# A hybrid encoder block on one core: one output run per half, independent stores in the inverse, head sums by two float32r products, and late places for two tiles

## The chip, the cores and the metric

The kernel runs on one core of a Trainium2 chip. The core has five engines, each with an instruction queue of its own that is worked in order: TensorE (PE, with its weight loads shown apart as PEld), VectorE (DVE), ScalarE (ACT), GpSimd (POOL) and SyncE (SP, which here only issues transfers). Engines wait for each other by semaphores. The metric is the device time of one execution in microseconds (us); lower is better.

## The reference

One layer of an encoder block on x of 1024 tokens by 1024 channels, in float32: two branches run side by side on the same normed input (stick-breaking attention and an RWKV-7 time mix), a gated merge, then a SwiGLU feed-forward part. The diff touches the time mix, 8 heads of 64 channels:

```python
kk = (k * k_k).reshape(B, S, H, N)
kk = kk / jnp.maximum(jnp.linalg.norm(kk, axis=-1, keepdims=True), 1e-12)   # a sum over a head
k = k * (1.0 + (a - 1.0) * k_a)
y = wkv7_scan(r_h, heads(decay), k_h, v_h, kk, heads(a))
mean = jnp.mean(y, axis=-1, keepdims=True)
var = jnp.mean(jnp.square(y - mean), axis=-1, keepdims=True)                # a sum over a head
y = ((y - mean) * lax.rsqrt(var + GN_EPS)).reshape(B, S, RW_WIDTH) * lnx_w + lnx_b
bonus = (jnp.sum(r_h * k_h * r_k, axis=-1, keepdims=True) * v_h)            # a sum over a head
return (y + bonus) * g
```

`wkv7_scan` steps a 64x64 state per head over the tokens: `sa = state @ -kk; state = state * w + sa (kk a)^T + v k^T; y = state @ r`.

## The kernel before

**Data.** Activations stand with channels on the 128 partitions and tokens along the rows. Products that need nearly float32 accuracy are made of three float32r products of parts: a value is cast to float32r (`hi`, on ACT) and the remainder taken (`lo = x - hi`, on DVE); `mm3` multiplies hi by hi, hi by lo, lo by hi.

**The time mix.** `rwkv` goes over four pairs of heads `p` (two heads fill 128 partitions) and two halves `hf` of 512 tokens: eight units. For each unit:

- `rw_elementwise` makes the operands from r, k, v. Two sums over each head, one for the norm of `kk` (`pn`) and one for the bonus (`pb`), are products with a 128x128 matrix of two blocks of ones (`b.ones`), in float32 with 512 columns. It masks products into `nx` (four chunks a tile), spreads v into `sv`, and copies blocks of it by DMA into `xv`.
- `rw_inverse` inverts a triangular 32x32 block per chunk, head and quarter: 31 steps of a multiply and a reduce on DVE (tiles `nl`, `ts`, `tm`), four stores of the result into a scratch in HBM (`td`), one load back in another order (`dt`), a 32x32 transpose on DVE, then small products on PE, 32 rows by 32 columns of the array, and 64 by 64 right after in `rw_elementwise`.
- `rw_chain` runs over eight chunks of 64 tokens. A chunk has two dependent 128x128 float32 products (`px`, then `ps`) with copies (`xv`), a scaled state (`sp`, on POOL) and the new state (`sv`, on DVE) between them. After chunks 3 and 7, four chunks' outputs are added into `y` by 8 products of 64x64 and 8 of 128x64, kept together.
- `rw_post` norms y, with a third sum over each head (`pn`), multiplies by the gate `g` loaded from HBM, and stores the half.

Projections for the next pair and gate tiles (`gate_tiles`) are recorded beside the chain as filler for PE: float32r products of 512 columns into PSUM tiles `d`.

**What sets the order.** Nothing runs in the order of the code. `Block` records every operation, and `schedule` lays them out by a list plan: each engine takes the able operation with the lowest priority number, at times that it reckons from `cost` and from `LATENCY` (from one engine's end to another's start), to which `wait` adds 80 ns between different engines. The finished order is what each engine's queue holds; the chip then waits only for semaphores. All instructions are issued from one helper line, L579 of the profile, so groups are told apart by tiles. An operation that must follow another is found by the boxes of memory that both touch (`regions`); for a scratch in HBM with strided boxes these may be wider than what is touched, so the four stores of `td`, which interleave, count as one after the other. For a transfer the planner reckons:

```python
    "sync": {"tensor": 2030, "vector": 2030, "scalar": 2030, "gpsimd": 2060, "sync": 2030},
...
    size = 4 * count(out.shape)
    return max(450.0, size / 360.0)
```

`choose` has a rule of its own for PE: after an operation that costs under 70 it prefers another such. These are small products; going from one array shape (rows x columns of the array in use) to another costs time, which `run` reckons by `array_mode` (INTO_PART 90, INTO_WHOLE 200). `together()` keeps a bundle's products adjacent.

**Places.** A tile gets a place of its class (`b`: 27 places of 1040 float32 per partition, each able to hold two small tiles) when the planner grants it. A tile may ask ahead of its turn within a window, 60 tiles for `b` or, with `near=True`, 12 (`PREFETCH`). A place that holds small tiles keeps in the profile the name of the one that took it first, so a sum's input may be listed as `b_gg`, `b_sh` or `b_tmp`.

Of the kernel before, what the change touches and what calls it, by code (L numbers as in the profile page):

```python
# [6 lines left out]
F32 = mybir.dt.float32  # L7
F32R = mybir.dt.float32r
BF16 = mybir.dt.bfloat16
AF = mybir.ActivationFunctionType  # L10
ALU = mybir.AluOpType
# [4 lines left out]
P = 128  # L16
# [3 lines left out]
H = 512  # L20
# [13 lines left out]
CH = 64  # L34
# [7 lines left out]
CC_ID, CC_CEN, CC_ONE, CC_MA, CC_TI, CC_SC, CC_N = 0, 128, 256, 384, 512, 768, 1280  # L42
# [214 lines left out]
class Block:  # L257
# [272 lines left out]
    def choose(self, able, waiting, at, last):  # L530


        import heapq

        if able[0][2].engine == "tensor" and waiting and waiting[0][3].steady:

            x = waiting[0]
            if x[0] <= at + 3 and x[1] < able[0][0]:
                heapq.heappop(waiting)
                return x[3]  # L540
        if able[0][2].engine == "tensor" and last is not None and last.cost < 70:
            short = [x for x in able if x[2].cost < 70]
            if short:
                pick = min(short)
                able.remove(pick)
                heapq.heapify(able)
                return pick[2]
        return heapq.heappop(able)[2]
# [59 lines left out]
    def proj(self, w, hf, cls="d"):  # L608
# [4 lines left out]
        return ps  # L613


    def rstd(self, srcs, junk):
# [25 lines left out]
def hybrid_block(tc, x, w_in, consts, params, rows, ups, gup, w_sb, w_rw, w_o, w_fg, w_fu, w_fd, out):  # L642
    b = Block(tc, {a.tensor.name for a in (x, w_in, consts, params, rows, ups, gup, w_sb, w_rw, w_o, w_fg, w_fu, w_fd)})
    nc = b
    T = b.t
    with ExitStack() as es:
# [8 lines left out]
        b.cls("sp", 3, CH)  # L655
        b.cls("q", 4, 256)
        b.cls("big", 4, 4 * S)
        for n in ("raw", "whi", "wlo"):
# [15 lines left out]
        for i, cls in enumerate("dd"):  # L674
            ps = T(cls, [P, H])
# [15 lines left out]
        b.cen = cst[:, CC_CEN : CC_CEN + P]  # L691
        b.ones = cst[:, CC_ONE : CC_ONE + P]
        b.mask_a = cst[:, CC_MA : CC_MA + P]
# [196 lines left out]
def rw_elementwise(b, u, p, hf, spill):  # L890
    nc = b.nc
    T = b.t
    pc, oka, cen, ones, mask_a, tinit = b.pc, b.oka, b.cen, b.ones, b.mask_a, b.tinit
    r, k, v = u["r"], u["k"], u["v"]
# [22 lines left out]
    nc.scalar.activation(t0[:], k[:], AF.Square, scale=pc(PC_KK + p))  # L917
    pn = T("e", [P, H])
    nc.tensor.matmul(pn[:], lhsT=ones, rhs=t0[:], start=True, stop=True)
    rn = T("b", [P, H], F32, "tmp")  # L920
# [22 lines left out]
    nc.vector.scalar_tensor_tensor(out=rk[:], in0=r[:], scalar=pc(PC_RK + p), in1=kp[:], op0=ALU.mult, op1=ALU.mult)  # L943
    pb = T("e", [P, H])
    nc.tensor.matmul(pb[:], lhsT=ones, rhs=rk[:], start=True, stop=True)
    bv = T("b", [P, H], F32, "bv")
# [36 lines left out]

    xv = T("b", [P, 8, P], F32, "xv")
    u["xv"] = xv
# [31 lines left out]
def rw_inverse(b, nd, nx, quads, tinit, p, hf):  # L1017
# [10 lines left out]
    for t in range(1, 32):  # L1028
        n = (t + 3) // 4
        nc.vector.tensor_tensor(out=tm[:, :n, : t + 1], in0=nl[:, None, 0 : t + 1, t].broadcast_to([P, n, t + 1]), in1=ts[:, :n, : t + 1], op=ALU.mult)  # L1030
        nc.vector.tensor_reduce(out=ts[:, :n, t], in_=tm[:, :n, : t + 1], axis=AX.X, op=ALU.add)
    td = b.scratch([32, 8, 4, 32], f"td{p}{hf}")
    for c in range(4):
        nc.sync.dma_start(td[:, :, c, :], ts[c:P:4])
    dt = T("q", [P, 8, 32])
    nc.sync.dma_start(dt[:], td.rearrange("(c a) j k t -> (a j k) c t", a=4))
# [26 lines left out]
def rw_chain(b, units, p, hf):  # L1063
# [6 lines left out]
    hs = [(0, slice(0, CH)), (1, slice(CH, P))]  # L1070
    y = None
    for c in range(8):
# [10 lines left out]
        if not last:  # L1083
# [3 lines left out]
            for h, rs in hs:  # L1087
                nc.vector.scalar_tensor_tensor(out=nsv[rs, ncx, rs], in0=ps[rs, rs], scalar=pl[rs, c : c + 1], in1=sp[rs, :], op0=ALU.mult, op1=ALU.add)
        if c % 4 == 3:
            g = c // 4  # L1090
            if y is None:
                y = u["y"] = T("y", [P, H])
            with b.together():
                for k in range(4 * g, c + 1):
                    for h, rs in hs:
                        nc.tensor.matmul(y[rs, k * CH : k * CH + CH], lhsT=sv[rs, k, rs], rhs=ar[rs, k, CH:P], start=k == 0, stop=False, skip_group_check=True)
                for k in range(4 * g, c + 1):
                    for h, rs in hs:
                        nc.tensor.matmul(y[rs, k * CH : k * CH + CH], lhsT=xv[:, k, rs], rhs=nx[g][:, k % 4, 1, h, :], start=False, stop=k == 7, skip_group_check=True)


def rw_post(b, u, p, hf, spill):
    nc = b.nc
    T = b.t
    pc, ones = b.pc, b.ones
    y, t0 = T("b", [P, H], F32, "ptmp"), T("b", [P, H], F32, "ptmp")
    nc.scalar.copy(y, u["y"])
    nc.scalar.activation(t0[:], y[:], AF.Square)
    pn = T("c", [P, H])
    nc.tensor.matmul(pn[:], lhsT=ones, rhs=t0[:], start=True, stop=True)  # L1110
    rs = T("b", [P, H], F32, "ptmp")
    nc.scalar.activation(rs[:], pn[:], AF.Ln, scale=1.0 / CH, bias=b.eps[:, 1:2])
    nc.scalar.activation(rs[:], rs[:], AF.Exp, scale=-0.5)
    nc.vector.scalar_tensor_tensor(out=rs[:], in0=y[:], scalar=pc(PC_LW + p), in1=rs[:], op0=ALU.mult, op1=ALU.mult)
    nc.vector.scalar_tensor_tensor(out=rs[:], in0=rs[:], scalar=pc(PC_LB + p), in1=u["bv"][:], op0=ALU.add, op1=ALU.add)
    g = T("b", [P, H], F32, "ptmp")
    nc.sync.dma_start(g[:], spill["g"][:])
    nc.gpsimd.tensor_tensor(out=rs[:], in0=rs[:], in1=g[:], op=ALU.mult)
    nc.sync.dma_start(b.orw_d[p][:, hf * H : hf * H + H], rs[:])
# [533 lines left out]
```

## Time and profile before

| | |
|---|---|
| Runs | 1610.81 us median of 3 (1609.73 to 1612.65) |
| Profiled execution | 1610.57 us, its span 1608.8 us |
| Instructions | 23912 |
| Granted TensorE clock | 0.999 mean |
| HBM | 129.27 MB read, 47.45 MB written, 110 GB/s over the span |

The rows are quoted in the prediction. In the table of groups, the columns are line, engine, operation, out<-in by the tiles' names, partitions x elements and type, count, then the busy time in us, the mean ns of one, and the engine's idle time just before them with what ended it. A matmul row has the array's rows x columns in use ahead of the shape. A float32 product is two records, a float32r one is one. A matmul's record runs from its start to its modelled end, so records of neighbours overlap: what a product takes of PE's time is read from the start of the next one.

### The profile page before, as it was taken

To read this page: it belongs to the slowest core of one execution; us is meant where nothing else is said; L and a number is where in the kernel's file an instruction comes from. 1 tells how busy PE (TensorE), PEld (TensorE's weight loads), DVE (VectorE), ACT (ScalarE), POOL (GpSimd) and SP (SyncE) were. 2 spreads that over 40 slices of the span, in tenths; PEclk is the share of its full clock that TensorE was granted. 3 is DMA by queue.
4 is the path that set the end of the run, shared out by engine and by line. 5 is a ranking of instruction groups with operands and counts; after the bars stand their busy time and mean duration, and the time that the engine had idled before them with its cause. 6 is when DMAs were issued, how large, how long until landed. Compare 5 with 4: busy or idle time off the path is not lost.

```text
span 1608.8 us, 23912 instructions
## 1 busy us (share of the span) xinstructions
PE 1586.0 (99%) x8932; PEld 1284.1 (80%) x8932; DVE 1128.0 (70%) x2004; ACT 716.5 (45%) x1401; POOL 254.5 (16%) x407
## 2 busy tenths in 40 slices
PE   9999999999999999999999999999999999999998
PEld 7877777777787888888787888888888888888876
DVE  7568689897864878895366349766666666867485
ACT  7533345444245766774444334323332332554352
POOL 1030233525233222230043110000000000000000
PEclk9999999999999999999999999999999999999999
DMA  5523233242321000003537112332232233874444
GB/s 214 203 88 92 79 100 86 59 140 83 105 71 40 27 27 27 27 27 122 180 118 274 66 40 81 116 98 98 99 111 89 95 111 124 310 240 144 136 152 183
DMA packets 106822, 180.38 MB, mean 112 GB/s; under 512 B 42321, under 2 KB 43345, under 8 KB 106706
## 3 DMA queue, kind: packets, MB, share of 16 engines
q1 hardware_dynamic: 106706, 178.85, 33.6%
q8 instruction: 70, 1.15, 0.3%
q14 instruction: 46, 0.38, 0.1%
HBM read 129.27 MB, written 47.45 MB: 110 GB/s over the span
## 4 chain that ended last, share of the span: by engine, by line
PE 86%; DVE 7%; ACT 3%; DMA 3%; issue 1%; POOL 0%; SPq 0%; DVEq 0%; ACTq 0%; POOLq 0%
PE d_d L579 39%; PE e_e L579 20%; PE c_c L579 16%; PE y_y L579 10%; DVE q_q L579 2%; DVE b_sv L579 1%; DMA b_wraw<-w_fd 0%; DVE big_h L579 0%; DVE b_xs L579 0%; ACT b_qst L579 0%; DMA q_q<-td 0%; DVE wlo_wlo L579 0%; DMA whi_oraw<-w_o 0%; DMA b_g<-gsc 0%; DVE b_nx L579 0%
## 5 line engine op out<-in xcount | busy, mean ns | idle before, releaser
L579 PE MATMUL d_d<-big_h,whi_whi 128*128 128x512 f32 x1280 | 434.5, 409 | 0.1
L579 PEld LDWEIGHTS d_d<-big_h,whi_whi 128*128 128x128 f32 x1280 | 234.9, 189 | 48.7 <-issue 5.5
L579 PE MATMUL d_d<-big_h,wlo_wlo 128*128 128x512 f32 x640 | 259.9, 406 | 0.0
L579 PEld LDWEIGHTS d_d<-big_h,wlo_wlo 128*128 128x128 f32 x640 | 120.7, 189 | 24.6 <-issue 2.4
L579 DVE TENSOR_TENSOR q_q<-b_nl,q_q 128x2 f32<-128x2 f32 (+30 forms) x248 | 86.5, 349 | 9.9 <-POOL b_sh L579 2.4
L579 ACT CAST whi_whi<-raw_raw 128x1024 fp32r<-128x1024 f32 (+1 forms) x60 | 55.9, 933 | 77.5 <-PE d_d L579 76.4
L579 DVE TENSOR_TENSOR_SCAN b_nb<-b_nb 128x128 f32<-128x128 f32 (+3 forms) x64 | 87.9, 1390 | 1.7 <-POOL b_nb L579 1.0
L579 DVE TENSOR_TENSOR wlo_wlo<-raw_raw,whi_whi 128x1024 fp32r<-128x1024 f32 (+1 forms) x60 | 69.5, 1160 | 27.4 <-ACT whi_whi L579 27.3
L579 POOL TENSOR_SCALAR sp_sp<-b_sv,pl_pl 64x64 f32<-64x64 f32 x120 | 63.3, 528 | 121.9 <-DVE b_sv L579 115.9
L579 ACT CAST b_wd<-b_wraw 128x512 fp32r<-128x512 f32 x70 | 42.1, 620 | 64.4 <-DVE b_wraw L579 30.0
L579 DVE TENSOR_REDUCE q_q<-q_q 128x1 f32<-128x2 f32 (+30 forms) x248 | 62.1, 250 | 6.8
L579 PE MATMUL d_d<-b_wd,big_act 128*128 128x512 f32 x264 | 66.5, 395 | 0.0
L579 PE MATMUL e_e<-b_wd,big_act 128*128 128x512 f32 x264 | 66.5, 394 | 0.0
L579 DVE TENSOR_TENSOR b_wd<-b_wraw,b_wd 128x512 fp32r<-128x512 f32 x70 | 46.4, 686 | 27.0 <-ACT b_wd L579 27.0
L579 POOL TENSOR_SCALAR_AFFINE_SELECT b_nb<-b_nb 128x128 f32<-128x128 f32 x64 | 45.4, 716 | 123.5 <-ACT b_nb L579 108.4
L579 PEld LDWEIGHTS e_e<-b_wd,big_act 128*128 128x128 f32 x264 | 49.6, 188 | 11.8
L579 PEld LDWEIGHTS d_d<-b_wd,big_act 128*128 128x128 f32 x264 | 49.6, 188 | 11.7
L579 DVE TENSOR_TENSOR b_wt<-c_c,b_wt 128x512 fp32r<-128x512 f32 (+2 forms) x96 | 50.0, 546 | 3.8 <-ACT b_wt L579 2.7
L579 ACT CAST b_wt<-c_c 128x512 fp32r<-128x512 f32 (+2 forms) x96 | 43.5, 481 | 20.5 <-PE c_c L579 19.5
L579 ACT COPY b_xv<-c_c 64x64 f32<-64x64 f32 x64 | 13.3, 207 | 86.2 <-DVE b_xv L579 46.0
L579 PE MATMUL c_c<-b_wd,big_act 128*128 128x512 f32 x198 | 50.8, 395 | 0.1
L579 PE MATMUL y_y<-b_wd,big_act 128*128 128x512 f32 x198 | 50.7, 394 | 0.0
(648 smaller groups left out, 3576.4 us busy)
## 6 DMA issues: line engine op xcount, KB each, us to landing
raw_raw<-w_in SPq DMA_DIRECT2D x42, 512.0 KB, 3.5
raw_raw<-w_fg SPq DMA_DIRECT2D x22, 512.0 KB, 3.5
raw_raw<-w_fu SPq DMA_DIRECT2D x22, 512.0 KB, 3.6
b_wraw<-w_fd SPq DMA_DIRECT2D x22, 512.0 KB, 4.7
act<-b_u SPq DMA_DIRECT2D x39, 256.0 KB, 3.1
b_x<-x SPq DMA_DIRECT2D x16, 512.0 KB, 9.0
b_mg<-gsc SPq DMA_DIRECT2D x28, 256.0 KB, 5.3
raw_araw<-act SPq DMA_DIRECT2D x14, 512.0 KB, 4.5
```

What stands on the lines that cost most here:

```text
L579: getattr(getattr(self.real, op.engine), op.method)(**kw)
```

## The change

1. `head_sums` replaces each of the three float32 products with the ones: the input is cast to float32r on ACT, the remainder taken on DVE, and two float32r products add into one PSUM tile. The ones themselves are copied once to float32r on ACT, at the start.
2. The outputs of a half are made in one bundle after chunk 7: 16 products of 64x64, then 16 of 128x64.
3. The four stores of `td` are taken out of each other's list of predecessors in the planner.
4. `xv` and the gate tile `g` get `near=True`.
5. `choose` prefers operations that use fewer than 128 rows of the array after one that did, in place of those that cost under 70.

```diff
-        if able[0][2].engine == "tensor" and last is not None and last.cost < 70:
-            short = [x for x in able if x[2].cost < 70]
+        if able[0][2].engine == "tensor" and last is not None and array_mode(last)[0] < P:
+            short = [x for x in able if array_mode(x[2])[0] < P]
...
+    def head_sums(self, cls, x):
+        nc = self.nc
+        both = self.t("b", [P, 2, H], F32R, "hs")
+        hi, lo = both[:, 0], both[:, 1]
+        nc.scalar.copy(hi, x)
+        nc.vector.tensor_tensor(out=lo, in0=x, in1=hi, op=ALU.subtract)
+        ps = self.t(cls, [P, H])
+        nc.tensor.matmul(ps, lhsT=self.ones, rhs=hi, start=True, stop=False)
+        nc.tensor.matmul(ps, lhsT=self.ones, rhs=lo, start=False, stop=True)
+        return ps
...
-        b.ones = cst[:, CC_ONE : CC_ONE + P]
+        b.ones = T("ones", [P, P], F32R)
+        nc.scalar.copy(b.ones, cst[:, CC_ONE : CC_ONE + P])
...
-    pn = T("e", [P, H])
-    nc.tensor.matmul(pn[:], lhsT=ones, rhs=t0[:], start=True, stop=True)
+    pn = b.head_sums("e", t0)
...
-    xv = T("b", [P, 8, P], F32, "xv")
+    xv = T("b", [P, 8, P], F32, "xv", near=True)
...
+    stores = set()
     for c in range(4):
         nc.sync.dma_start(td[:, :, c, :], ts[c:P:4])
+        b.ops[-1].preds -= stores
+        stores.add(b.ops[-1])
...
-        if c % 4 == 3:
-            g = c // 4
-            if y is None:
-                y = u["y"] = T("y", [P, H])
-            with b.together():
-                for k in range(4 * g, c + 1):
...
+    y = u["y"] = T("y", [P, H])
+    with b.together():
+        for k in range(8):
...
-    g = T("b", [P, H], F32, "ptmp")
+    g = T("b", [P, H], F32, "ptmp", near=True)
```

(`pb` in `rw_elementwise` and `pn` in `rw_post` change as `pn` above.)

The first head sum of the first unit on PE, among projections. `d_d` is a projection's output, `big_h` the normed input, `whi` and `wlo` a weight's parts; `b_gg` is here the place of the squared k. Before:

```order
L579 MATMUL d_d_967<-big_h_200,whi_whi_863 128x512
L579 MATMUL d_d_967<-big_h_214,whi_whi_863 128x512
L579 MATMUL d_d_967<-big_h_200,wlo_wlo_871 128x512
L579 MATMUL e_e_997<-b_gg_721,cst_cst_146 128x512
L579 MATMUL d_d_1001<-big_h_192,whi_whi_934 128x512
L579 MATMUL d_d_1001<-big_h_208,whi_whi_934 128x512
```

After:

```order
L579 MATMUL d_d_974<-big_h_202,whi_whi_868 128x512
L579 MATMUL d_d_974<-big_h_216,whi_whi_868 128x512
L579 MATMUL d_d_974<-big_h_202,wlo_wlo_876 128x512
L579 MATMUL e_e_1005<-b_hs_859,ones_ones_166 128x512 x2
L579 MATMUL d_d_1010<-big_h_194,whi_whi_941 128x512
L579 MATMUL d_d_1010<-big_h_210,whi_whi_941 128x512
```

The sum stands at the same place, as two products with the float32r ones.

The first outputs of the first chain on PE (`b_ar`, `b_sv`, `b_nx`, `b_xv` as above). Before, after chunk 3; rows of the same two forms stand again after chunk 7:

```order
L579 MATMUL d_d_1843<-big_h_208,whi_whi_1658 128x512
L579 MATMUL c_c_1849<-b_xv_1053,b_bkt_1202 128x128
L579 MATMUL y_y_1852<-b_ar_915,b_sv_1010 64x64 x8
L579 MATMUL y_y_1852<-b_nx_1158,b_xv_1053 64x64 x8
L579 MATMUL d_d_1843<-big_h_192,wlo_wlo_1670 128x512
L579 MATMUL c_c_1881<-b_sv_1010,b_nx_1184 128x128
```

After, once, behind chunk 7:

```order
L579 MATMUL d_d_1959<-big_h_194,whi_whi_1879 128x512
L579 MATMUL c_c_1985<-b_xv_1053,b_bkt_1239 128x128
L579 MATMUL y_y_1989<-b_ar_922,b_sv_1020 64x64 x16
L579 MATMUL y_y_1989<-b_nx_1179,b_xv_1053 64x64 x8
L579 MATMUL y_y_1989<-b_nx_1219,b_xv_1053 64x64 x8
L579 MATMUL d_d_1959<-big_h_210,whi_whi_1879 128x512
```

Two runs have become one of double length.

The fifth inverse's transfers on SP (`td` the scratch, `q_q` the inverse's tiles, `gsc` gates, `raw` weights, `orw` a half's result). Before:

```order
L579 DMA td_120<-q_q_2845 256x1x32 x2
L579 DMA orw_83<-b_ptmp_1004 128x512
L579 DMA gsc_70<-b_tmp_3678 128x512
L579 DMA td_120<-q_q_2845 256x1x32
L579 DMA raw_raw_3762<-w_in 128x1024
L579 DMA td_120<-q_q_2845 256x1x32
L579 DMA b_tmp_3678<-g_d_107 128x512
L579 DMA gsc_71<-b_tmp_3682 128x512
L579 DMA q_q_3800<-td_120 128x8x32
```

After:

```order
L579 DMA raw_raw_3842<-w_in 128x1024
L579 DMA gsc_72<-b_k_2162 128x512
L579 DMA td_120<-q_q_2880 256x1x32 x4
L579 DMA gsc_72<-b_pp_2608 128x512
L579 DMA q_q_3925<-td_120 128x8x32
L579 DMA raw_raw_3929<-w_in 128x1024
```

Four stores stand in a row, and one gate's store between them and the load.

More of the change, by code (lines that the diff above doesn't have):

```diff
@@ L656, in hybrid_block @@
         b.cls("q", 4, 256)
+        b.cls("ones", 1, P)
         b.cls("big", 4, 4 * S)
@@ L892, in rw_elementwise @@
     T = b.t
-    pc, oka, cen, ones, mask_a, tinit = b.pc, b.oka, b.cen, b.ones, b.mask_a, b.tinit
+    pc, oka, cen, mask_a, tinit = b.pc, b.oka, b.cen, b.mask_a, b.tinit
     r, k, v = u["r"], u["k"], u["v"]
@@ L943, in rw_elementwise @@
     nc.vector.scalar_tensor_tensor(out=rk[:], in0=r[:], scalar=pc(PC_RK + p), in1=kp[:], op0=ALU.mult, op1=ALU.mult)
-    pb = T("e", [P, H])
-    nc.tensor.matmul(pb[:], lhsT=ones, rhs=rk[:], start=True, stop=True)
+    pb = b.head_sums("e", rk)
     bv = T("b", [P, H], F32, "bv")
@@ L1070, in rw_chain @@
     hs = [(0, slice(0, CH)), (1, slice(CH, P))]
-    y = None
     for c in range(8):
@@ L1088, in rw_chain @@
                 nc.vector.scalar_tensor_tensor(out=nsv[rs, ncx, rs], in0=ps[rs, rs], scalar=pl[rs, c : c + 1], in1=sp[rs, :], op0=ALU.mult, op1=ALU.add)
-        if c % 4 == 3:
-            g = c // 4
-            if y is None:
-                y = u["y"] = T("y", [P, H])
-            with b.together():
-                for k in range(4 * g, c + 1):
[L1095 to L1099, printed above, removed]
+    y = u["y"] = T("y", [P, H])
+    with b.together():
+        for k in range(8):
+            for h, rs in hs:
+                nc.tensor.matmul(y[rs, k * CH : k * CH + CH], lhsT=sv[rs, k, rs], rhs=ar[rs, k, CH:P], start=k == 0, stop=False, skip_group_check=True)
+        for k in range(8):
+            for h, rs in hs:
+                nc.tensor.matmul(y[rs, k * CH : k * CH + CH], lhsT=xv[:, k, rs], rhs=nx[k // 4][:, k % 4, 1, h, :], start=False, stop=k == 7, skip_group_check=True)
 def rw_post(b, u, p, hf, spill):
@@ L1104, in rw_post @@
     T = b.t
-    pc, ones = b.pc, b.ones
+    pc = b.pc
     y, t0 = T("b", [P, H], F32, "ptmp"), T("b", [P, H], F32, "ptmp")
@@ L1108, in rw_post @@
     nc.scalar.activation(t0[:], y[:], AF.Square)
-    pn = T("c", [P, H])
-    nc.tensor.matmul(pn[:], lhsT=ones, rhs=t0[:], start=True, stop=True)
+    pn = b.head_sums("c", t0)
     rs = T("b", [P, H], F32, "ptmp")
```

## The prediction

> **What bounds the kernel now.** I read the page's busy shares and its chain first, then the busy time by stage, then who TensorE (PE) waited for, and last the timeline at the places that the diff touches.
>
> ```profile
> span 1608.8 us, 23912 instructions
> PE 1586.0 (99%) x8932; PEld 1284.1 (80%) x8932; DVE 1128.0 (70%) x2004; ACT 716.5 (45%) x1401; POOL 254.5 (16%) x407
> PE 86%; DVE 7%; ACT 3%; DMA 3%; issue 1%; POOL 0%; SPq 0%; DVEq 0%; ACTq 0%; POOLq 0%
> ```
>
> PE is busy for 99% of the span, and the chain that ended last runs over PE for 86% of it. What leaves PE's queue shortens the program unless a wait takes its place; what leaves another engine's does not. The stages, in a table of windows whose columns are the stretch, its length, and the busy time of PE, PEld, DVE, ACT and POOL:
>
> ```profile
> 0.00:89.00 89.00, 84.87 (x464) 68.39 (x465) 55.25 (x67) 55.95 (x101) 10.05 (x36) 1.00 0.57 203
> 89.00:540.00 451.00, 442.74 (x3545) 349.95 (x3544) 353.89 (x912) 191.63 (x410) 144.90 (x270) 1.00 0.29 83
> 540.00:760.00 220.00, 219.21 (x1282) 186.82 (x1281) 178.51 (x246) 145.27 (x324) 55.66 (x78) 1.00 0.13 40
> 760.00:1609.00 849.00, 839.17 (x3648) 678.99 (x3646) 540.37 (x781) 323.65 (x566) 43.92 (x24) 1.00 0.40 137
> ```
>
> All that the diff edits, but for the copy of the ones at the start, lies between 89 and 540 us. There PE stood still for 451.00 - 442.74 = 8.3 us, beside a vector engine (DVE) that is busy 78% of the time. From the merge on PE's rows stand in the same order before and after, so I carry the last stretch over. The granted clock is 1.00 throughout and I leave it there. Of the waits, these matter (waiting, waited for, sum, times, longest):
>
> ```profile
> PE e_e L579 <- DVE b_nx L579: 2.3, 1, 2.3
> PE c_c L579 <- DVE b_sv L579: 2.2, 5, 0.7
> ...
> PE c_c L579 <- ACT b_xv L579: 1.4, 3, 0.6
> ...
> PE y_y L579 <- DVE q_q L579: 1.0, 2, 0.7
> ```
>
> They are small and scattered: the chain of chunks and the inverse are long, but the planner lays projections between their products, so PE seldom sees them. The sum is made against the profiled execution, 1610.57 us (span 1608.8 and 1.8 around it), which lies 0.24 us under the median of the three runs, 1610.81. A measurement of this kernel can tell about 0.2%, 3.2 us, from no change.
>
> **Head sums: 24 float32 products of 512 columns become 48 float32r ones.** There are three sums per half (two in `rw_elementwise`, one in `rw_post`), and 4 pairs of 2 halves. On PE's timeline (start, us, row):
>
> ```profile
> 200.84 0.38 PE L579 MATMUL e_e<-cst_cst,b_bk 128*128 128x128 f32 x2
> 201.06 1.02 PE L579 MATMUL c_c<-b_sh,cst_cst 128*128 128x512 f32 x2
> 201.92 0.38 PE L579 MATMUL e_e<-cst_cst,b_bk 128*128 128x128 f32 x2
> ...
> 209.47 0.86 PE L579 MATMUL d_d<-big_h,whi_whi 128*128 128x512 f32 x3
> 210.16 0.39 PE L579 MATMUL d_d<-big_h,wlo_wlo 128*128 128x512 f32 x1
> ```
>
> One float32 sum is two records, and the next product starts 201.92 - 201.06 = 0.86 us after it. The projections are float32r products of the same shape: three of them take 210.16 - 209.47 = 0.69 us, 0.23 each. Two cost 0.46, so a sum gives back 0.40, and 24 give **-9.6 us**. Both products have the same weights in float32r, as all projections have, and I see no row from which they would run slower than a projection.
>
> **The halves' outputs in one run.** Before, each half has two runs of small products (chunks 0 to 3, 4 to 7):
>
> ```profile
> 185.58 0.38 PE L579 MATMUL c_c<-b_xv,b_bkt 128*128 128x128 f32 x2
> 185.89 0.68 PE L579 MATMUL y_y<-b_ar,b_sv 64*64 64x64 f32 x16
> 186.50 0.69 PE L579 MATMUL y_y<-b_nx,b_xv 128*64 128x64 f32 x16
> 187.12 0.50 PE L579 MATMUL d_d<-big_h,wlo_wlo 128*128 128x512 f32 x1
> L579 PE MATMUL y_y<-b_ar,b_sv x256: 217/218/268, 185.9 to 507.9; 64*64 64x64 f32 x128
> ```
>
> The product before is as long as the pair at 200.84, 0.22, so it would be followed at 185.80; the run starts at 185.89 and pays 0.09 for going over to small arrays. It ends at 187.12: 1.32 us in all. The last of the 16 records of a kind starts 0.68 - 0.22 = 0.46 after the first (0.22 is one record's median), so a record takes 0.03 and 16 more of a kind 0.49. One run of double length costs 1.32 + 2 x 0.49 = 2.30 against 2 x 1.32 = 2.64; eight halves give **-2.7 us**. The output of chunks 0 to 3 is now made some 10 us later; nothing reads it before `rw_post`, which already waited for chunk 7. The altered rule in `choose` merges or parts a few other runs: PE's order has three changes of array fewer beside those above, some 0.1 each, which I count as nothing.
>
> **The inverse's transfers.** They take no PE time. On SP's queue, DVE and PE, around the fifth inverse:
>
> ```profile
> 340.72 1.22 SPq L579 DMA_DIRECT2D td<-q_q  x2
> ...
> 345.36 0.52 SPq L579 DMA_DIRECT2D td<-q_q  x1
> ...
> 348.17 0.52 SPq L579 DMA_DIRECT2D td<-q_q  x1
> ...
> 351.55 0.37 SPq L579 DMA_DIRECT2D q_q<-td  x1
> ...
> DMA to landing us min/median/max: 1.9/2.4/3.9
> ...
> 354.55 1.22 DVE L579 TENSOR_TENSOR wlo_wlo<-raw_raw,whi_whi 128x1024 fp32r<-128x1024 f32 x1
> 355.68 0.44 DVE L579 STREAM_TRANSPOSE q_q<-q_q 128x256 f32<-128x256 f32 x1
> ...
> 356.27 0.69 PE L579 MATMUL y_y<-q_q,b_nx 32*32 32x32 f32 x32 [0.38 <-DVE q_q L579]
> ```
>
> Now the load goes out 10.83 us after the first store, though the stores wait for nothing of each other: the planner only thought so and put other transfers between them. In a row four take 4 x 0.61 = 2.4 to issue, the last goes out at 1.8 and lands 2.4 (median) later, at 4.2. So the inverse is ready some 6.6 us earlier. PE, which ran projections meanwhile, gains nothing from that directly. But PE's queue is in order, and the planner moves the inverse's products up by as much as it believes to have won. It books 0.45 + 2.03 a transfer: 4 x 2.48 + 2.56 = 12.5 us before, 4 x 0.45 + 2.03 + 2.56 = 6.4 now. By the rows it is 10.8 + 2.4 to 3.9 = 13.2 to 14.7 before, and 4.2 + 2.4 to 3.9 = 6.6 to 8.1 now. It was late by 0.7 to 2.2 and will be late by 0.2 to 1.7, or more where the load stands behind another transfer that waits: in the new order a gate's store stands there in this same place. Eight inverses cost PE 1.0 us now. The bounds are 0 and 8 x 1.7 = 13.6; I take twice what the rows show, 2.0, as the lateness is no larger: **+1.0 us**.
>
> **The casts and subtractions.** Each sum adds one of each:
>
> ```profile
> L579 ACT CAST b_wd<-b_wraw 128x512 fp32r<-128x512 f32 x70 | 42.1, 620 | 64.4 <-DVE b_wraw L579 30.0
> L579 DVE TENSOR_TENSOR b_wd<-b_wraw,b_wd 128x512 fp32r<-128x512 f32 x70 | 46.4, 686 | 27.0 <-ACT b_wd L579 27.0
> L579 POOL TENSOR_SCALAR sp_sp<-b_sv,pl_pl x120: 435/443/1461, 89.1 to 504.7; 64x64 f32<-64x64 f32 x120
> ...
>   POOL sp_sp L579: 1.0, 1
> ```
>
> 24 x 0.62 = 14.9 us on ACT and 24 x 0.69 = 16.5 on DVE. ACT has 451 - 192 = 259 us free in the stage. DVE goes from 353.9 of 451 to 370.4 of some 440, 78% to 84%. They are hidden by the products that the planner lays between; if that cover fails, PE waits up to 0.62 + 0.69 = 1.31 a sum. The ends are 0 and 31 us; the nearest row is PE's waiting for DVE and ACT in the stage, 8.3 us under a load of 78%, which I let grow a little more than the load: **+1.0 us**. GpSimd (POOL) works beside DVE. Its `sp` product of the chain takes 0.44 us at the median and 1.46 at most, so something holds it up now and then, but DVE waited for it once, 1.0 us in all; from that row I add nothing. [...]
>
> **The rest.** The copy of the ones comes second on ACT, before the two small steps of the first row norm:
>
> ```profile
> 6.17 0.20 ACT L579 ACTIVATE tiny_tiny<-tiny_tiny 128x1 f32<-128x1 f32 x1
> 6.40 0.69 DVE L579 COPY b_b<-d_d 128x512 f32<-128x512 f32 x1 [1.01 <-PE d_d L579]
> 7.18 1.29 DVE L579 SCALAR_TENSOR_TENSOR b_xs<-b_x,tiny_tiny,b_b 128x1024 f32<-128x1024 f32 x1
> ```
>
> A quarter of a 128x512 cast's columns costs at most its 0.62; the norm is then ready at 6.99, and DVE is with its copy until 7.09: nothing. The two tiles with late places put `xv` and the gate `g` later on SP; `xv` is first needed by a chain that starts only after the inverse, `g` only by POOL's last product of a half, on which the merge waits 200 us later: nothing, while these covers last.
>
> Sum: -9.6 - 2.7 + 1.0 + 1.0 = -10.3, so 1600.3; I say **1600.5 us**.
>
> **Rivals.** *The new subtraction stands before the chain (slower).* DVE's queue is in order too:
>
> ```profile
> 124.14 0.16 DVE L579 TENSOR_TENSOR q_q<-b_nl,q_q 128x2 f32<-128x2 f32 x1 [2.38 <-POOL b_sh L579]
> ...
> 126.52 1.16 PE L579 MATMUL e_e<-cst_cst,b_sg 128*128 128x128 f32 x8 [2.27 <-DVE b_nx L579]
> ```
>
> Here an early step of the inverse held DVE for 2.38 us, the mask product `nx` stood behind it, and PE lost 2.27. If each of 24 subtractions, or the hold-up of POOL beside it, pushes a chain step back by its own 0.69, PE pays 16.5: 1610.6 - 12.3 + 16.5 = 1614.8. It decides from 12.3/24 = 0.51 us a sum. Against it: in the same stage DVE makes dozens of such subtractions of double length for weights, and PE's whole wait there is 8.3.
>
> *The inverse's cover is cut.* Eight products late by 1.2 on average instead of 0.13: +8.6 over now, 1610.6 - 12.3 + 8.6 + 1.0 = 1607.9, and with the bound of 13.6 the gain is gone. For it: the load stands behind other transfers. Against it: lateness was larger before.
>
> *The whole saving and fewer waits.* The single 2.27 at 126.5 and the inverse's 1.0 do not recur: 1610.6 - 12.3 - 3.3 = 1595.0. The orders differ from 89 us on, so it is open which waits recur.
>
> **Chances.** Forecast, 1597.5 to 1604: 0.60. Fewer waits, under 1597.5: 0.17. Inverse late, 1604 to 1607.5: 0.13; the same to the full, about no change: 0.06. Subtraction before the chain, slower: 0.04. The range 1594.5 to 1606.5 leaves out the last two, half of the inverse's case and a little below: under 0.2. Faster by more than 0.2%: 0.90, within 0.06, slower 0.04.
>
> **What would show it.** Right: PE's busy time between 89 and 540 us falls by some 12; a pair of `ones` products takes 0.46; eight output runs of 2.2 us; four stores in a row and the load 4 to 5 us after the first; PE's wait for DVE `q_q` at 1 to 3 us in all. Wrong: PE waiting for DVE `hs`, for `q_q` or for `b_sv` by more than 5 us each, or a new wait for weights because SP is held by stores in a row.

## The result, and the profile after

The changed kernel takes 1613.84 us, median of 21 runs (1611.21 to 1619.86), against 1610.83 us for the kernel before in 21 runs beside it (1608.89 to 1613.1). The ratio is 1.0020, 95% interval 1.0014 to 1.0027: slower by about as much as can be told from no change. I had forecast 1600.5, at most 1606.5. The profiled execution took 1613.76 us, its span 1611.9. From its page:

```profile
span 1611.9 us, 23965 instructions
PE 1580.7 (98%) x8932; PEld 1285.4 (80%) x8932; DVE 1135.7 (70%) x2028; ACT 728.9 (45%) x1426; POOL 254.2 (16%) x407
PE 80%; DVE 10%; DMA 4%; ACT 2%; issue 2%; SPq 1%; POOL 0%; DVEq 0%; ACTq 0%; POOLq 0%
```

PE is busy for 5.3 us less than before, but the chain that ended last runs over PE for 80% of the span instead of 86%, and over DMA and DVE for more. The windows by stage (stretch, length, busy time of PE, PEld, DVE, ACT, POOL, granted clock):

```profile
0.00:89.00 89.00, 84.96 (x462) 69.14 (x463) 56.30 (x69) 57.10 (x104) 10.73 (x35) 0.98 0.53 194
89.00:540.00 451.00, 433.35 (x3497) 345.69 (x3496) 347.94 (x916) 194.92 (x406) 137.62 (x263) 0.99 0.30 84
540.00:763.00 223.00, 222.52 (x1325) 190.71 (x1324) 190.16 (x264) 153.12 (x350) 61.12 (x87) 1.00 0.13 41
763.00:1612.00 849.00, 839.93 (x3654) 679.86 (x3652) 541.27 (x781) 323.81 (x567) 44.76 (x24) 1.00 0.39 137
```

In the time mix PE stands still for 451.00 - 433.35 = 17.7 us instead of 8.3, and the clock, 1.00 before, is 0.99 there and 0.98 in the first stage. Who PE waited for:

```profile
PE y_y L579 <- DVE q_q L579: 8.2, 7, 1.9
PE e_e L579 <- DVE b_nx L579: 2.5, 3, 1.8
...
PE c_c L579 <- ACT b_nx L579: 1.6, 1, 1.6
PE c_c L579 <- DVE b_xv L579: 1.6, 5, 0.5
...
PE c_c L579 <- DVE b_hs L579: 0.9, 1, 0.9
PE c_c L579 <- DVE b_sv L579: 0.8, 2, 0.5
```

The first row is most of it: PE waits for the loaded and transposed inverse (`q_q`) in seven halves of eight, 8.2 us, where it waited twice for 1.0 before. That is 7.2 of the 9.4 us added. The new sums (`b_hs`) cost 0.9 here, and 1.4 with two smaller rows that are not shown. The fifth inverse on SP, DVE and PE:

```profile
360.87 3.36 SPq L579 DMA_DIRECT2D td<-q_q  x4
364.33 0.55 SPq L579 DMA_DIRECT2D gsc<-b_pp  x1
365.72 0.38 SPq L579 DMA_DIRECT2D q_q<-td  x1
...
360.43 0.41 DVE L579 TENSOR_REDUCE q_q<-q_q 128x8 f32<-128x256 f32 x1
...
368.22 0.45 DVE L579 STREAM_TRANSPOSE q_q<-q_q 128x256 f32<-128x256 f32 x1 [3.40 <-DMA q_q<-td]
...
368.73 0.69 PE L579 MATMUL y_y<-q_q,b_nx 32*32 32x32 f32 x32 [1.70 <-DVE q_q L579]
```

From the end of the last step (360.84) to the transpose it is 7.4 us, booked 6.4; PE, which had its projections laid out for the booked time, stands still for 1.70. Last, the clock, in four windows of 3.4 us around the sixth inverse, and its mean over the span:

```profile
405.50:408.90 3.40, 3.40 (x26) 2.42 (x25) 2.61 (x5) 1.32 (x2) 0.13 (x1) 1.00 0.29 45
408.90:412.30 3.40, 1.34 (x8) 0.86 (x7) 1.40 (x3) 0.58 (x1) 1.15 (x1) 1.00 0.38 59
412.30:415.80 3.50, 3.41 (x40) 3.06 (x41) 0.73 (x2) 1.61 (x4) 1.57 (x4) 0.51 0.37 108
415.80:419.20 3.40, 3.40 (x19) 2.66 (x18) 1.82 (x4) 3.29 (x8) 0.00 (x0) 1.00 0.47 182
```

Between 408.9 and 412.3 PE is busy for 1.34 us of 3.40; in the next 3.4 us it works at half clock. The trace has four such stretches of 3.41 us, starting at 33.5, 118.8, 412.4 and 470.4 us (and one at the end of the program, as before has). Each costs 1.7 us of PE's speed. These waits of PE stand ahead of them:

```profile
33.50 4.72 PE L579 MATMUL d_d<-big_h,b_b 128*128 128x256 f32 x25 [2.06 <-DVE b_sh L579]
...
118.92 1.12 PE L579 MATMUL e_e<-cst_cst,b_bk 128*128 128x128 f32 x4 [1.82 <-DVE b_nx L579]
...
412.39 1.07 PE L579 MATMUL y_y<-q_q,b_nx 32*32 32x32 f32 x32 [1.93 <-DVE q_q L579]
...
468.46 0.49 PE L579 MATMUL c_c<-b_sv,b_nx 128*128 128x128 f32 x2 [1.62 <-ACT b_nx L579]
469.51 0.70 PE L579 MATMUL d_d<-big_h,whi_whi 128*128 128x512 f32 x2 [0.56 <-DVE b_kst L579]
```

The two at 412.4 and 470.4 follow waits that are new: 1.93 us for the inverse, and 1.62 and 0.56 us for ACT and DVE. The two at 33.5 and 118.8 follow waits of 2.1 and 1.8 us that the kernel before has as well (2.1, and 2.3 at 126.5 us), behind which its profiled execution kept its clock. Over all runs the mean clock is 0.995, that of the kernel before 0.998.

The account of the profiled executions: PE's work is its busy time less 1.7 us for each such stretch, 1586.0 before and 1580.7 - 4 x 1.7 = 1573.9 after. That is -12.1, close to the forecast (-12.3); the table below shows that kernels with the same work differ by up to 4.3 us in this figure. The idle time of the time mix takes back 9.2 and the clock 6.8 in this execution (0.003 of 1612 us, 4.8, in the mean of all); the sum, +3.9, is within 1 us of the 3.2 between the two executions.

### The profile page after: what moved, and what is told of

Read it like the earlier page. It is cut to its first block, busy times and chain, and to the rows that moved or that the text cites. A ratio compares the mean times of both kernels' runs of the same rounds, so it can differ in the third digit from the quotient of the medians.

```text
span 1611.9 us, 23965 instructions
## 1 busy us (share of the span) xinstructions
PE 1580.7 (98%) x8932; PEld 1285.4 (80%) x8932; DVE 1135.7 (70%) x2028; ACT 728.9 (45%) x1426; POOL 254.2 (16%) x407
## 4 chain that ended last, share of the span: by engine, by line
PE 80%; DVE 10%; DMA 4%; ACT 2%; issue 2%; SPq 1%; POOL 0%; DVEq 0%; ACTq 0%; POOLq 0%
PE d_d L579 35%; PE e_e L579 18%; PE c_c L579 17%; PE y_y L579 11%; DVE q_q L579 3%; DMA q_q<-td 1%; SPq L579 1%; DMA b_wraw<-w_fd 1%; DVE b_nx L579 1%; DVE b_nb L579 1%; DVE b_sv L579 1%; DMA td<-q_q 1%; DVE b_xs L579 1%; DVE wlo_wlo L579 0%; DVE big_h L579 0%
## 5 line engine op out<-in xcount | busy, mean ns | idle before, releaser
L579 PE MATMUL d_d<-big_h,whi_whi 128*128 128x512 f32 x1280 | 428.7, 406 | 0.8 <-DVE b_kst L579 0.6
L579 PEld LDWEIGHTS d_d<-big_h,whi_whi 128*128 128x128 f32 x1280 | 235.8, 189 | 45.0 <-PE c_c L579 0.7
L579 PE MATMUL d_d<-big_h,wlo_wlo 128*128 128x512 f32 x640 | 260.7, 408 | 0.1
L579 PEld LDWEIGHTS d_d<-big_h,wlo_wlo 128*128 128x128 f32 x640 | 121.2, 190 | 23.1 <-DVE wlo_wlo L579 0.4
L579 DVE TENSOR_TENSOR q_q<-b_nl,q_q 128x2 f32<-128x2 f32 (+30 forms) x248 | 87.7, 354 | 10.7 <-PE y_y L579 4.3
L579 ACT CAST whi_whi<-raw_raw 128x1024 fp32r<-128x1024 f32 (+1 forms) x60 | 55.9, 933 | 86.8 <-PE d_d L579 85.8
L579 DVE TENSOR_TENSOR_SCAN b_nb<-b_nb 128x128 f32<-128x128 f32 (+3 forms) x64 | 85.5, 1356 | 2.6 <-POOL b_nb L579 2.4
L579 DVE TENSOR_TENSOR wlo_wlo<-raw_raw,whi_whi 128x1024 fp32r<-128x1024 f32 (+1 forms) x60 | 70.2, 1171 | 22.3 <-ACT whi_whi L579 16.5
L579 POOL TENSOR_SCALAR sp_sp<-b_sv,pl_pl 64x64 f32<-64x64 f32 x120 | 62.2, 518 | 117.9 <-DVE b_sv L579 112.1
L579 ACT CAST b_wd<-b_wraw 128x512 fp32r<-128x512 f32 x70 | 41.9, 620 | 63.2 <-DVE b_wraw L579 28.5
L579 PE MATMUL d_d<-b_wd,big_act 128*128 128x512 f32 x264 | 66.6, 395 | 0.0
L579 PE MATMUL e_e<-b_wd,big_act 128*128 128x512 f32 x264 | 66.5, 394 | 0.0
L579 DVE TENSOR_REDUCE q_q<-q_q 128x1 f32<-128x2 f32 (+30 forms) x248 | 61.9, 250 | 6.4
L579 DVE TENSOR_TENSOR b_wd<-b_wraw,b_wd 128x512 fp32r<-128x512 f32 x70 | 46.2, 686 | 26.3 <-ACT b_wd L579 26.3
L579 PEld LDWEIGHTS d_d<-b_wd,big_act 128*128 128x128 f32 x264 | 49.6, 188 | 11.8
L579 PEld LDWEIGHTS e_e<-b_wd,big_act 128*128 128x128 f32 x264 | 49.6, 188 | 11.7
L579 POOL TENSOR_SCALAR_AFFINE_SELECT b_nb<-b_nb 128x128 f32<-128x128 f32 x64 | 40.9, 647 | 110.3 <-ACT b_nb L579 109.6
L579 PE MATMUL y_y<-b_wd,big_act 128*128 128x512 f32 x198 | 50.8, 395 | 0.1
L579 DVE TENSOR_TENSOR b_wt<-c_c,b_wt 128x512 fp32r<-128x512 f32 (+2 forms) x96 | 49.8, 545 | 1.5 <-ACT b_wt L579 0.4
L579 PE MATMUL c_c<-b_wd,big_act 128*128 128x512 f32 x198 | 50.8, 395 | 0.0
L579 ACT CAST b_wt<-c_c 128x512 fp32r<-128x512 f32 (+2 forms) x96 | 43.6, 482 | 9.7 <-PE c_c L579 8.6
L579 ACT COPY b_xv<-c_c 64x64 f32<-64x64 f32 x64 | 13.3, 207 | 75.7 <-PE c_c L579 48.9
```

Source lines behind the costliest of these rows:

```text
L579: getattr(getattr(self.real, op.engine), op.method)(**kw)
```

## The experiments

Each run is measured beside runs of the kernel before on its own chip, whose medians lie between 1609.57 and 1610.68 us. The plan's end is what the planner reckons by its own costs while it lays the program out; idle is PE's from 89 to 560 us; half is the number of half-clock windows of 3.41 us before the program's last stretch; work is PE's busy time less 1.7 us for each.

| kernel | plan's end | us | ratio, 95% | idle | half | work |
|---|---|---|---|---|---|---|
| before | 1599.1 | 1610.83 | | 8.4 | 0 | 1586.0 |
| changed | 1590.9 | 1613.84 | 1.0014-1.0027 | 17.7 | 4 | 1573.9 |
| e1 stores ordered | 1619.4 | 1639.09 | 1.0171-1.0198 | 27.3 | 11 | 1571.7 |
| e2 load booked later | 1606.9 | 1627.11 | 1.0095-1.0123 | 20.8 | 11 | 1572.7 |
| e3 stores only | 1603.7 | 1620.48 | 1.0058-1.0083 | 13.1 | 2 | 1588.2 |
| e4 sums only | 1615.0 | 1634.32 | 1.0142-1.0170 | 24.9 | 8 | 1576.9 |
| e5 run only | 1603.1 | 1614.31 | 1.0017-1.0035 | 13.4 | 2 | 1581.4 |
| e15 places, choice | 1600.4 | 1613.64 | 1.0014-1.0033 | 9.3 | 1 | 1586.8 |
| e10 changed, replanned | 1587.0 | 1605.32 | 0.9946-0.9972 | 12.3 | 0 | 1575.8 |
| e17 the same, other | 1587.2 | 1608.89 | 0.9979-0.9997 | 15.4 | 2 | 1573.2 |
| e11 before, replanned | 1599.1 | 1613.54 | 1.0003-1.0023 | 6.7 | 2 | 1588.2 |
| e12 before, margin | 1604.7 | 1625.11 | 1.0067-1.0095 | 16.5 | 5 | 1586.2 |
| e9 some waits filled | 1590.9 | 1614.97 | 1.0017-1.0036 | 11.5 | 3 | |
| e13 all waits filled | 1590.9 | 1610.23 | 0.9992-1.0011 | 10.0 | 2 | |
| e14 e2, waits filled | 1606.9 | 1626.47 | 1.0094-1.0122 | 15.0 | 4 | |
| e16 inverse early | 1590.9 | 1603.38 | 0.9943-0.9969 | 10.5 | 2 | 1576.0 |

### One part at a time

The first four undo or do one part. In the changed kernel, the stores counted one after the other again (e1):

```diff
-        b.ops[-1].preds -= stores
-        stores.add(b.ops[-1])
```

> The changed kernel with one part undone: the planner again counts the inverse's four stores as one after the other. Theory A (moving the inverse's products up left PE waiting for them, and the waits cost clock besides): PE's wait for DVE q_q falls from 8.2 us to 1 to 2, most of the half-clock stretches go (the profile of the change has four of 3.41 us after the start, 1.7 us lost in each), the work saved stays: 1613.8 - 7 - 5 = about 1602, below the kernel before by 7 to 11 us. Rival B (the added subtractions make DVE late, and the inverse's transpose only stands behind them; the stores are innocent): q_q still waits 5 us or more, 1610 to 1614.

The load of the inverse booked 2 us later, where `late` is added to the time from which the planner takes an operation to be ready (e2):

```diff
     nc.sync.dma_start(dt[:], td.rearrange("(c a) j k t -> (a j k) c t", a=4))
+    b.ops[-1].late = 2000
```

> The changed kernel with its independent stores, but the planner books the inverse's load as landing 2 us later than it did (nothing else changes; the transfers themselves are the same). Theory A: the products stand some 2 us later on PE, which covers the lateness of 0 to 2.4 us that the profile shows; q_q waits under 1.5 us, the clock is full but for the start, 1599 to 1604. Rival B: the subtractions' lateness is elsewhere, waits for b_hs, b_sv and b_nx stay at 5 us or more and the time at 1608 or above.

In the kernel before, the edit of the stores alone (e3), and the three sums alone (e4):

```diff
+        b.ops[-1].preds -= stores
+        stores.add(b.ops[-1])
```

> The kernel before with the stores' part of the change alone. Theory A: PE gains no work and pays the lateness of eight inverses: q_q waits 5 to 9 us, some stretches at half clock, 1616 to 1624, slower. Rival B: without the subtractions DVE is on time, q_q waits about 1 us, 1608 to 1612. Third view (an earlier inverse helps the chain): under 1608.

```diff
-    pn = T("e", [P, H])
-    nc.tensor.matmul(pn[:], lhsT=ones, rhs=t0[:], start=True, stop=True)
+    pn = b.head_sums("e", t0)
```

> The kernel before with the head sums' part of the change alone. Theory A: 24 sums cheaper by 0.40 us, waits little changed, full clock: 1601 to 1604. Rival B: the casts and subtractions cost PE waits of 5 us or more for b_hs and what stands behind them, 1606 or above.

The two later ones of this kind, the output run alone (e5), and the late places and the rule in `choose` (e15):

> The kernel before with one part of the change, the output of a half in one run of 64 small products. Planned end 1603.1 against 1599.1 us, with gaps of 1.9, 1.7 and 1.6 us on TensorE. The prediction's term is -2.7 us of TensorE's work: the net (span less TensorE's idle time and lost clock) should be 1587 to 1589 us against 1590.5. The time goes by the plan that comes of it: theory A 1610 to 1620 us. If the run's place were what cost the change its gain (products held back to the end of the chain, so that TensorE has less to do inside it), idle in the recurrence rises by 5 us or more over 8.4, as with the change.

> The kernel before with the two smallest parts of the change, the late places of two tiles and the altered choice among small products. The prediction counts both as nothing. Planned end 1600.4 against 1599.1 us, largest gap 0.8 us. Net work 1589 to 1591 us, and a time of 1609 to 1614 us. Above 1616 us, or a wait of TensorE for one of the two tiles of 1 us or more, the parts that I costed at nothing have a price of their own.

Five of six have medians above both kernels', and the parts do not add up to the whole. The times of e1, e2 and e4 miss their expectations by 23 us and more; those of e3, e5 and e15 lie inside theirs. In e3 the stores alone raised PE's wait for `q_q` from 1.0 to 4.6 us, a little under the 5 to 9 expected. The longest waits of PE in e1, e2 and e4, one view each (L579 reads L580 and more in kernels with lines added above it):

```profile
PE d_d L579 <- DVE b_tmp L579: 9.7, 1, 9.7
```

```profile
PE y_y L580 <- issue: 3.4, 2, 2.2
PE e_e L580 <- DVE b_nx L580: 2.6, 3, 1.9
PE c_c L580 <- DVE b_xv L580: 2.3, 4, 1.0
...
PE y_y L580 <- DVE q_q L580: 1.0, 1, 1.0
```

```profile
PE d_d L579 <- DVE b_ptmp L579: 3.6, 1, 3.6
PE y_y L579 <- issue: 3.3, 1, 3.3
PE c_c L579 <- DVE b_sv L579: 2.9, 5, 0.9
```

Each has long waits at places that its edit does not touch. Most of them stand in the plan already: the plan of e1 leaves PE idle for 9.5 us at 271 us, that of e4 for 3.4 and 3.8 at 268 and 280. An edit of one operation makes the planner lay out all later ones anew, and where the filler runs short inside a chain depends on the whole order. In e2 the waits for `q_q` fell from 8.2 to 1.0 as expected, and the time rose by 13 us. So a part tried alone measures its new plan more than the part. Only the work column is steady: with sums and run 1572 to 1576, with neither 1586 to 1588, with the sums alone 1576.9 (-9.1; forecast -9.6), with the run alone 1581.4 (-4.6; forecast -2.7, which is about as close as this reckoning comes). In e5 the idle time rose by 4.9 us, close to the 5 that its expectation names as the sign that holding the outputs back costs PE its filler. e12 below gains 8.0 us of idle time by a new plan alone, so e5 does not decide this; e16, which has the long runs in the changed kernel's order, has 10.5 us of idle time against 8.4 before, so there some 2 us at most can be theirs. The 3.8 us that e15 lost beside its own runs of before (1609.8) are only half in its profile, 2.1, of which 1.7 is one half-clock window; they are within what a new plan costs, and so the two parts that I took for nothing are neither confirmed nor priced.

### The same work in another plan

To test that directly: the kernel before with one constant of the planner changed (e12), and both kernels with bookings chosen for a plan without gaps that a later load would not tear open (e10, e17 the changed kernel, e11 the one before).

```diff
-MARGIN = 80
+MARGIN = 75
```

> The kernel before with one constant of the planner changed and no instruction: each wait between two engines is booked 0.075 instead of 0.08 us above its latency. Planned end 1604.7 us against 1599.1, with gaps on TensorE of 2.5 and 2.1 us at 467 and 546 us. Rival N, which by now is part of theory A (a plan is a throw of its own): 1615 to 1625 us, 5 to 14 above before, with the net work of TensorE the same 1590 us. If plans differ little on the chip: 1609 to 1613.

```diff
-PREFETCH = 12
+PREFETCH = 8
-MARGIN = 80
+MARGIN = 90
...
     nc.sync.dma_start(dt[:], td.rearrange("(c a) j k t -> (a j k) c t", a=4))
+    b.ops[-1].late = 900
```

> The changed kernel, with the same instructions, laid out by other bookings: the inverse's load booked 0.9 us later, each wait between two engines booked 0.09 instead of 0.08 us above its latency, and a tile may claim its place 8 instead of 12 places ahead of its turn. Planned end 1587.0 us against 1590.9, with no gap on TensorE above 0.51 us in the recurrence (the changed kernel's plan has one of 2.3). Theory A (the work is worth 13 us, and waits that the plan did not book and the clock that follows them ate it): TensorE's idle in the recurrence falls from 17.6 to 8 to 12 us, lost clock from 10.3 to 3 to 6, and the time is 1595 to 1602 us. Rival B (the edits themselves cost on the chip, the new copies and subtractions above all, in whatever order): waits on those tiles stay and the time stays above 1608. Rival N (a plan's end tells nothing of the chip's): anything up to 1630 us, as with the four plans before.

> The changed kernel, with the same instructions, laid out by other bookings once more: the inverse's load 1.5 us later, places claimed 8 ahead, waits booked as in the changed kernel. Planned end 1587.2 us. A reckoning of the plan with stores of 0.6 us and a load 0.5 to 2.5 us later than planned has it within 2 us of the plan that gave 1605.32. Theory A: idle in the recurrence 8 to 13 us, mean clock 0.997 or more, 1602 to 1609 us. Rival N (the good plan was one lucky throw): 1610 to 1630.

> The kernel before, with the same instructions, laid out by other bookings found in the same way: the inverse's load 0.9 us later, 0.085 us, 16 places. Planned end 1599.1 us, as before. Theory A: the kernel before has little to win, since its waits in the recurrence are small (8.3 us of idle) and its lost clock 2.3 us: 1603 to 1610 us; the distance to the changed kernel in its new plan is then the work, some 10 us. If new bookings alone made the gain, this one gains as much as the changed kernel does, 12 us or more. Rival N: anything from 1600 to 1630.

Five nanoseconds in the planner's margin cost the kernel before 14.4 us (1625.11 against 1610.68 beside it) with its work unchanged. It waits most for two results of DVE:

```profile
PE e_e L579 <- DVE b_nx L579: 5.6, 3, 3.0
PE d_d L579 <- DVE b_kst L579: 2.5, 1, 2.5
```

The changed kernel has better plans: e10 is 8.5 us faster than it and 0.4% faster than before, the fastest complete kernel here, with no half-clock window. It missed its expected 1595 to 1602 by 3.3 us all the same, and 2.3 us of waits for `q_q` are left in it. e17, with other bookings, gains 4.9. The kernel before did not gain from such bookings (e11 missed its expectation of 1603 to 1610). From e11 to e10 it is 8.2 us, from e12 to the changed kernel 11.3; each such distance holds two plans, and only the work column is free of them.

### The clock, with the order kept

Here the order of the changed kernel is kept to the last instruction, and products that nobody reads are put inside PE's waits after planning: 58 short ones into three waits (e9), then 48 of 0.25 us into all eight waits of 0.9 us and more before 502 us (e13). `FILL` counts the products ahead of an operation. The diff is cut from e13; e9 puts its products in by a field of the operation and writes them to the place that the waiting product will write.

```diff
             for op in self.schedule():
+                for _ in range(FILL.get(op.seq, 0)):
+                    self.real.tensor.matmul(dst, lhsT=one, rhs=one, start=True, stop=True)
```

> The changed kernel in its own order, to the last instruction, with 58 products of the ones tile by itself (128x128, float32r, some 0.06 us each, results overwritten) put in after the planning: 20 ahead of the transposes that waited 1.82 us at 118.92, 20 ahead of the 32x32 run that waited 1.93 us for the inverse at 412.39, 18 ahead of the product that waited 1.62 us at 468.46. They stand inside waits that stay, so no work moves. Theory A (a grid window of 3.41 us in which TensorE rests for 1.7 us or more is followed by one at half clock, 1.7 us lost each): the half-clock stretches at 118.8, 412.4 and 470.4 go, three times 1.7 us, and the span is some 5 us shorter, 1607 and a time of 1609 us; the idle of TensorE falls by 3.4 us while the waits' ends stay. Rival C (the low clock comes of something else, heat or the load as a whole): the stretches stay or move elsewhere, and the time stays at 1613 to 1615 us, or rises by up to 1 us where a filled wait is shorter than its products.

> The changed kernel in its own order, with 48 products by themselves (the constants' first 128 columns by themselves, float32, 128x128, some 0.2 us each, into a place of the accumulators that nobody uses at the time) put in after the planning, inside each of the eight waits of TensorE of 0.9 us and more between 33 and 502 us that its profile shows, 0.3 to 0.5 us shorter than the wait. No other work is added, and unlike in the try before they stand ahead of waits for places too. Theory A (a window of 3.41 us with 1.7 us of rest is followed by one at half clock): no window of the stretch keeps 1.7 us of rest, all half-clock stretches ahead of the last stage go, the mean clock rises from 0.995 to that of the kernel before, 0.998, and with it the time falls by some 4 us, to 1609 to 1611. Rival C (the low clock has another cause): clock 0.995 and 1613 to 1616 us.

e9 missed: 1614.97 us, clock 0.995. The products at 118.9 stood behind the wait instead of in it, since that wait is for the place they write to, and waits of 2.1 us (ending at 34.2) and 1.9 us (at 167.5) were left open; its profile has half-clock windows behind these two and behind the one that had been at 118.9. At its two other places the clock stayed full. e13, which writes to a free place, fills all eight: its mean clock over 11 runs is 0.998 and its time 1610.23, 3.6 us below the changed kernel with more work for PE (3.1 us by the ratios, each beside its own runs of before). The sixth inverse there, the products (L583) ahead of the small ones, then the windows:

```profile
410.15 1.73 PE L583 MATMUL y_y<-cst_cst 128*128 128x128 f32 x14
411.80 0.69 PE L587 MATMUL y_y<-q_q,b_nx 32*32 32x32 f32 x32
```

```profile
408.40:411.80 3.40, 3.16 (x24) 2.59 (x22) 1.79 (x4) 0.59 (x1) 1.92 (x3) 1.00 0.57 132
411.80:415.20 3.40, 3.40 (x50) 3.06 (x50) 1.64 (x4) 2.78 (x7) 0.94 (x3) 1.00 0.38 99
```

The window that had been at 0.51 is at 1.00, and the half-clock stretch is gone; the profile has two others, at 129.7 and 774.8, behind waits of the unfilled kind. So the cause of the low clock is PE's rest, and 3.1 to 3.6 us of the changed kernel's time were that. The fill covers the waits at 33.5 and 118.9 too, which the kernel before has; that one reaches 0.998 with them open, so most of the gain should belong to the new waits, but no run fills these alone. The same fill in e2:

> The kernel of the second try (the load booked 2 us later; 1627.11 us, clock 0.988, 20.7 us of lost clock) in its own order, with 57 such products inside its waits of 0.45 us and more between 33 and 560 us. Theory A: its lost clock falls from 20.7 to below 8 us, the mean clock rises to 0.995 or more, and the time falls to 1613 to 1619 us (less than the clock won, where the chain and not TensorE sets the pace): then most of the distance between this plan and the planner's own time for it was clock. Rival C: clock and time stay, 0.988 and 1625 to 1630.

Its clock rose from 0.989 to 0.994, but the time fell by 0.6 us only (1627.11 to 1626.47), so it missed the expected 1613 to 1619. In e2 PE rests for 5.3 of the 37.5 us of its half-clock windows, for results of DVE and ACT among others, so part of the slower products may have gone into waits that were there anyway. That was not tested, and why so little was won stays open; what remains of e2's loss goes with its plan.

### The inverse, with the order kept

Again the changed kernel's order, with every instruction and its length. The sums of the last two steps of each inverse are written to an unused tile, so the inverse lacks its last two rows; the stores need not wait for those two steps (e16).

```diff
+        if t >= 30:
+            b.ops[-1].aside = n
...
+                if op.aside:
+                    kw["out"] = self.junk[:, 0 : op.aside]
```

> The changed kernel in its own order on every engine, with every instruction and its length kept; only the sums of the last two of 31 steps of each inverse are written to an unused tile (so the inverse lacks its last two rows). The stores of the inverse then need not wait for these two steps, which stand on VectorE between other work: in the first half they end at 155.3 us and the step before them at 149, so that the load comes 2 to 5 us sooner. Theory A (the lateness of the inverse is paid one to one, and the clock on top): TensorE's wait for the inverse falls from 8.2 us to below 1.5, its idle time in the recurrence from 17.6 to 9 to 12 us, the two half-clock stretches that go with these waits leave, mean clock 0.996 to 0.997, and the time falls by 8 to 11 us to 1603 to 1606 us. Rival D (another wait stands right behind, for the chain's parts or for ScalarE, and takes over): the waits for the inverse go as well, but idle time stays at 15 us or more and the time at 1609 to 1614.

It takes 1603.38 us: 10.5 less than the changed kernel (10.3 by the ratios), with the same products in the same order. Its fifth inverse, then its waits, then its row for 89 to 560 us, below it that of the changed kernel:

```profile
353.24 2.54 SPq L583 DMA_DIRECT2D td<-q_q  x4
...
363.32 0.69 PE L583 MATMUL y_y<-q_q,b_nx 32*32 32x32 f32 x32
```

```profile
PE e_e L583 <- DVE q_q L583: 1.2, 1, 1.2
...
PE y_y L583 <- DVE q_q L583: 0.4, 2, 0.2
```

```profile
89.00:560.00 471.00, 460.46 (x3672) 368.94 (x3671) 375.38 (x952) 219.06 (x463) 157.68 (x282) 0.99 0.27 81
```

```profile
89.00:560.00 471.00, 453.35 (x3613) 362.50 (x3612) 366.72 (x942) 211.59 (x445) 150.71 (x280) 0.99 0.28 81
```

The waits for the inverse fall from 8.2 to 0.4, with 1.2 at another product behind, and PE's idle time from 17.7 to 10.5: no other wait takes their place. 7.1 us of idle time, from the profiled executions, and 0.0016 of clock (0.9950 to 0.9966 in the mean of all runs, 2.6 us) make 9.7 of the 10.5. The edit brings the inverse sooner than the planner had booked it, so it shows what the waits cost and is not a cure.

## Why the prediction was wrong

**Right: the work.** -12.3 forecast, -12.1 seen, in a figure that scatters by a few us from plan to plan. Each of the eight output runs takes 2.0 us from its first start to its last and 0.15 behind it, as forecast. The new casts and subtractions made PE wait some 1.4 us for `b_hs` (0.9 at DVE's longest), +1.0 forecast; the rival in which each subtraction pushes the chain back did not come. GpSimd was held up no more beside the new subtractions: `sp` takes 0.44 us at the median and 1.44 at most, 0.44 and 1.46 before, and DVE waited 1.2 us for it in all, 1.0 before.

**Wrong: the term for the inverse's transfers, +1.0 taken, +7.2 seen.** The lateness I had nearly right. I gave 0.2 to 1.7 us a half; over the eight the transpose comes 6.4 to 8.8 us after the last step, mean 7.5, against 6.4 booked, so it is 0.0 to 2.4 us late. The failed step is "as the lateness is no larger". I took PE's wait before, 1.0, for the price of that lateness. But before, the transpose came 12.3 to 15.0 us after the last step, mean 13.4, against 12.5 booked: 0.9 late on average too, and PE waited in only the two halves where it was 14.5 and 15.0. In those two halves it waited 0.7 and 0.4 us, so 1.3 to 2.1 us of lateness were covered by the products that stood ahead in PE's queue. In the new plan the inverse's products stand about at the booked time, and PE waits in seven halves. The lateness sums to 9.1 us over the eight, and PE waits 8.2; in a single half the wait is up to 0.9 us shorter or 0.7 longer than the lateness, so the match is one of the sums. e16 shows that these waits were paid: without them, in the same order, the idle time is 7.1 us shorter. The bound of 13.6 and the rival with the cut cover (+8.6) had the mechanism and its size; I gave them 0.19.

**Wrong: "The granted clock is 1.00 throughout and I leave it there."** That was a row of before, and I carried it into a kernel with longer rests. In the profiled execution two of the new waits are followed by half-clock windows, and over all runs the clock is 0.003 lower, 4.8 us; e13 won 3.1 to 3.6 us of time by filling the long waits. I had no term and no rival for it.

**Not seen: the plan as a whole.** I summed parts, and noted that it is open which waits recur. e12 shows that a plan alone moves this kernel by 14 us, so the forecast's range of 12 us was narrower than what it left open. In this case the rest of the plan was not the main cause: the two named terms, 7.2 - 1.0 + 3.1 to 4.8, explain 9 to 11 of the 13.3 us missed, and e16, with the order kept, comes to within 3 us of the forecast although the waits ahead of 33.5 and 118.8 stay in it. The last 2 to 4 us are not accounted for term by term.

## What to carry over

Where a planner books a transfer shorter than the chip takes, the price of moving its consumer up can come near the whole difference, summed over its uses, even where PE hardly waited before (here 8.2 us of waits for 9.1 of lateness, against 1.0); compare the booked with the traced time from producer to consumer over all uses, not the wait of one. A part of a change can't be priced by trying it alone when every edit lays the program out anew: keep the finished order and change one time in it (e13, e16), and read PE's work apart from its idle time. Beside its own length a wait can cost clock: in these traces no window with less than 1.37 us of PE's rest was followed by one at half clock, and all with 1.9 us or more were, at 1.7 us each.

## What the runs showed of the hardware

TensorE's clock was halved after windows with as little as 1.37 us of rest, and on a fixed grid. In the 14 traces that have half-clock stretches ahead of the program's end they are whole windows of 3.413 us, on a grid that starts at another place in each execution; the changed kernel's second, third and fourth start 85.3, 378.9 and 436.9 us after its first, 25, 111 and 128 windows. I counted the windows at full clock of all 16 traces up to the last stretch (in the other two the grid is laid by the start of that stretch). All 28 in which PE rested for 1.9 us or more in sum were followed by one at half clock; so were 8 of the 15 with 1.71 (half a window) to 1.9 us, 5 of the 55 with 1.0 to 1.71 us, the shortest rest being 1.37, and none with less. In the changed kernel's profile PE rested for 2.05, 1.72, 2.13 and 2.03 us in the windows ahead of its four; in that of the kernel before, windows with 1.81 and 1.79 us of rest (from 32.57 and 124.73 us) were followed by full clock. So a wait of 1.8 us cost 1.7 us more or nothing: the one that ended at 118.92 us lay with 1.72 of its 1.82 us in one window, and the next ran at half clock. Three waits of the changed kernel cost nothing more in the profiled execution: those ending at 164.64 and 368.73 us, 1.8 and 1.7 us long, lay over an edge, and the one at 501.12, 1.55 us, inside a window. This may be a part of the spread of the changed kernel's runs: 1611.2 to 1613.8 us at a clock of 0.996 or 0.997, 1615.9 to 1619.9 at 0.993.
